# A shorter attention softmax, gate weights in the score buffers, and an instruction order chosen from sixteen

## The chip, the cores and the metric

The kernel runs on one core of a Trainium2 chip. The metric is the device time of one execution in microseconds; before the change it is 1131.54 us, the median of three runs (1131.02 to 1131.56). The engines have names in the profile: PE is TensorE (PEld its weight loads), DVE is VectorE, ACT is ScalarE, POOL is GpSimd, and SP is SyncE, whose queue issues all DMAs of this kernel.

## The reference

One inference step of a decoder with two layers, for a prompt of 512 tokens and eight samples of one token, all in float32. Layer 0 is a gated linear recurrence (HGRN2) with 16 heads of 128; layer 1 is sliding-window attention with 32 query heads of 64, four key and value heads, a window of 128 and a sink per head. Each layer ends with a gate on a per-layer embedding. The attention of the prompt, cut to its core:

```python
def sink_softmax(s, sinks):
    sink = sinks.astype(jnp.float32).reshape(KV_HEADS, Q_PER_KV)[:, :, None, None]
    sink = jnp.broadcast_to(sink, s.shape[:-1] + (1,))
    pr = jax.nn.softmax(jnp.concatenate([s, sink], axis=-1), axis=-1)
    return pr[..., :-1]

    def one_block(args):
        qn, kn, vn, n = args
        mask = in_band & ((cidx >= WINDOW) | (n > 0))
        s = jnp.einsum('bqhgd,bkhd->bhgqk', qn.astype(jnp.float32), kn.astype(jnp.float32)) * ATTN_SCALE
        s = jnp.where(mask, s, -jnp.inf)
        pr = sink_softmax(s, sinks)
        return jnp.einsum('bhgqk,bkhd->bqhgd', pr, vn.astype(jnp.float32))
...
        h = h + rmsnorm(mix, post_norm_g[l])
        h = h + (p[l] @ w_pe[l]) * jax.nn.sigmoid(h @ w_pg[l])
```

## The kernel before

Activations lie transposed: 128 features on the partitions, 520 tokens (512 of the prompt, 8 samples) in a row. A float32 matmul is made of three products of a high and a low half: `wh` and `wl` are the halves of a weight tile of 128 x 512, made by a cast on ACT and a subtraction on DVE (or POOL) from the raw tile `wr`, which a DMA loads. `stream` runs through all projection tiles; `piece` loads a raw tile of 128 x 1024 (tag `wr`, two buffers) and splits half of it. A projection tile is accumulated in `pj`, a pair of PSUM banks, two buffers; all other matmuls use the four banks `ph`.

The attention is computed in eight units of four query heads; each unit has four blocks of 128 queries (`block`, line 1153 on). In a block, PE makes the scores of 128 queries against up to 256 keys (`ph<-xr,g`, keys in `xr`, split queries in `g`), ACT copies one half of the keys and DVE lays the other half over it under a mask, so that 128 scores per query remain in the tile `W` (printed as `b`, in the buffers `b3` or `b2`). Then comes the softmax: a maximum (`an`), three small instructions with the sink, exponentials with an accumulated sum (`ad`), one exponential of the sink (`ae`), an addition, a reciprocal and a multiply. PE transposes `W` (`ph<-ident,b`), ACT and DVE split the result into `g`, and PE multiplies it with the values (`ph<-g,b`). The halves of the result lie on different partitions and are added into `ao`, by way of a copy `m`. Around the blocks PE has the projections of later units and the output projections of earlier ones (`pj<-xs` and `pj<-og`). After units 3 and 7 the attention of the samples runs (`sample_b`, tiles `qs`, `bd`, `bm`).

The gate tiles (`gates`) take pairs of weight tiles; every second pair is marked `spare`, and its halves go to the buffers `b4` of the recurrent layer's state instead of `wh` and `wl`. Its raw tile was still a `wr`.

The order of all this is not written by hand. Every operation is recorded by `enter` with a price, and `issue` (line 200 on) is a list scheduler: engine by engine it takes the ready operation that can start first by its prices and hand-off times, with main work ranked against side work, and puts it into the program. Each engine then works through its own queue in that order; a late operand holds back all that is behind it in the same queue. All instructions carry the line of the helper that records them, 162, so the groups are told apart by tile names.

Of the kernel before, what the change touches and what calls it, by code (L numbers as in the profile page):

```python
# [18 lines left out]
P = 128  # L19
# [12 lines left out]
NEG = -1.0e30  # L32
# [24 lines left out]

WINDOW, LOADS = 1200, 400
# [11 lines left out]
class Slots:  # L70


    def __init__(self, tag, bufs):
        self.free = [0.0] * bufs
        self.keep = next((k for t, k in KEEP.items() if tag == t), max(1, bufs // 2))
        self.order, self.at = [], 0


class Plan:
# [120 lines left out]
    def issue(self):  # L200
        clock = dict.fromkeys(("tensor", "vector", "scalar", "gpsimd", "sync"), 0.0)
# [60 lines left out]
        while todo:  # L262
# [8 lines left out]
            self.tc.keep_in_program_order(op.calls[n]())  # L271
# [46 lines left out]
        self.end = max(clock.values())  # L318
# [39 lines left out]
class Step:  # L358
# [53 lines left out]
    def more_consts(self):  # L412
        nc, cp, i = self.nc, self.cp, self.i
        self.ident = cp.tile([P, P], F32, name="ident")
        nc.sync.dma_start(self.ident, i["ident"])
        self.pairmask = cp.tile([P, 64], F32, name="pairmask")
        nc.sync.dma_start(self.pairmask, i["pairmask"])
        self.ones_r = cp.tile([P, P], F32R, name="ones_r")
        nc.scalar.copy(self.ones_r, self.ones.to_broadcast([P, P]))
        self.lmask = self.plan.tile(self.sp, [P, 6, 64], I32, "lmask", "m", 1)  # L420
        nc.sync.dma_start(self.lmask.rearrange("p a b -> p (a b)"), i["lmask"])
        self.neg = cp.tile([P, 1], F32, name="neg")
        nc.vector.memset(self.neg, NEG)
# [64 lines left out]
    def piece(self, order, n):  # L488
# [76 lines left out]
    def rsqrt_small(self, ps, rows, cols, n, tag):  # L565
        nc = self.nc
        ms = self.small(tag + "m", [P, 8])
        nc.vector.tensor_scalar(ms[:rows, :cols], ps, 1.0 / n, EPS, op0=ALU.mult, op1=ALU.add)
        r = self.small(tag + "r", [P, 8])
# [521 lines left out]
    def unit_proj(self, u, xs, st, done):  # L1091
# [61 lines left out]
    def block(self, u, st, n, osb):  # L1153
# [6 lines left out]
        W = self.small("b3", [P, 4, P], 2) if n % 3 else self.small("b2", [P, 4, P], 3)  # L1160
        for a in range(2):
# [5 lines left out]
            w = W[:, 2 * a : 2 * a + 2]  # L1167
            if n == 0:
# [4 lines left out]
                    self.neg.unsqueeze(1).to_broadcast([P, 2, P]),  # L1173
# [453 lines left out]
```

## Time and profile before

| what | value |
|---|---|
| median of three runs | 1131.54 us |
| profiled execution | 1133.34 us |
| its span, first to last instruction | 1131.5 us |
| mean granted PE clock | 0.995 |
| DMA, mean over the span | 122 GB/s |
| HBM read, written | 119.22 MB, 16.77 MB |

The profiled execution took 1.8 us more than the span that its records cover. The granted clock is the share of full speed that TensorE was allowed; it is 1.00 nearly everywhere. By the 40 slices of the page the recurrent layer fills the time to about 590 us, its norm, gates and the keys and values the time to 690 us, the attention that to 1040 us, and the rest is output projection, norm and gates.

### The profile page before, as it was taken

To read this page: it belongs to the slowest core of one execution; us is meant where nothing else is said; L and a number is where in the kernel's file an instruction comes from. 1 tells how busy PE (TensorE), PEld (TensorE's weight loads), DVE (VectorE), ACT (ScalarE), POOL (GpSimd) and SP (SyncE) were. 2 spreads that over 40 slices of the span, in tenths; PEclk is the share of its full clock that TensorE was granted. 3 is DMA by queue.
4 is the path that set the end of the run, shared out by engine and by line. 5 is a ranking of instruction groups with operands and counts; after the bars stand their busy time and mean duration, and the time that the engine had idled before them with its cause. 6 is when DMAs were issued, how large, how long until landed. Compare 5 with 4: busy or idle time off the path is not lost.

```text
span 1131.5 us, 23984 instructions
## 1 busy us (share of the span) xinstructions
PE 1106.6 (98%) x8999; PEld 1088.3 (96%) x8999; DVE 966.1 (85%) x2218; ACT 749.7 (66%) x1990; POOL 121.8 (11%) x188
## 2 busy tenths in 40 slices
PE   8999999999999999999999999999989999999998
PEld 7999999999999999999999999999989999999997
DVE  6998888758888588888879989999988998998983
ACT  7878777657775477777736657767666764764551
POOL 0121121112211122111100000110100000000000
PEclk9999999999999999999999999999989999999999
DMA  8433524334432343434445442212212222312532
GB/s 292 150 135 115 187 99 170 110 136 152 139 126 97 118 165 134 143 125 138 141 151 204 127 152 91 77 57 86 84 39 75 76 75 75 107 49 73 205 104 86
DMA packets 53821, 137.56 MB, mean 122 GB/s; under 512 B 10948, under 2 KB 18124, under 8 KB 53704
## 3 DMA queue, kind: packets, MB, share of 16 engines
q1 hardware_dynamic: 53704, 136.02, 35.7%
q8 instruction: 71, 1.16, 0.4%
q14 instruction: 46, 0.38, 0.1%
HBM read 119.22 MB, written 16.77 MB: 120 GB/s over the span
## 4 chain that ended last, share of the span: by engine, by line
PE 70%; DVE 20%; ACT 5%; issue 3%; DMA 1%; POOLq 0%; SPq 0%; POOL 0%; DVEq 0%; ACTq 0%
PE pj L162 56%; PE ph L162 14%; DVE g L162 4%; DVE tmp L162 3%; DVE wl L162 3%; DVE b L162 2%; ACT b L162 1%; DVE ao L162 1%; DVE an L162 1%; DVE xr L162 1%; DMA wr<-in_w_pg 1%; DVE x L162 1%; ACT tmp L162 1%; ACT g L162 1%; ACT wh L162 1%
## 5 line engine op out<-in xcount | busy, mean ns | idle before, releaser
L162 PE MATMUL pj<-xs,wh 128*128 128x260 f32 x3328 | 571.2, 285 | 0.8 <-DVE x L162 0.3
L162 PEld LDWEIGHTS pj<-xs,wh 128*128 128x128 f32 x3328 | 468.9, 189 | 4.1 <-ACT xs L162 1.2
L162 PE MATMUL pj<-xs,wl 128*128 128x260 f32 x1664 | 346.6, 285 | 0.0
L162 PEld LDWEIGHTS pj<-xs,wl 128*128 128x128 f32 x1664 | 260.7, 189 | 0.8
L162 ACT CAST wh<-wr 128x512 fp32r<-128x512 f32 x288 | 176.3, 618 | 97.9 <-PE pj L162 87.0
L162 DVE TENSOR_TENSOR wl<-wr,wh 128x512 fp32r<-128x512 f32 x273 | 188.1, 692 | 31.3 <-ACT wh L162 29.9
L162 PE MATMUL pj<-og,wh 128*128 128x260 f32 x1056 | 187.3, 287 | 2.5 <-ACT g L162 1.4
L162 PEld LDWEIGHTS pj<-og,wh 128*128 128x128 f32 x1056 | 152.9, 190 | 4.7 <-DVE x L162 1.8
L162 PE MATMUL pj<-og,wl 128*128 128x260 f32 x512 | 108.0, 286 | 0.0
L162 ACT ACTIVATE tmp<-pj 128x520 f32<-128x520 f32 (+1 forms) x93 | 48.0, 528 | 55.0 <-PE pj L162 54.5
L162 PEld LDWEIGHTS pj<-og,wl 128*128 128x128 f32 x512 | 81.3, 190 | 0.6
L162 ACT ACTIVATE sb<-sb,nv 128x128 f32<-128x128 f32 x128 | 68.4, 564 | 0.2
L162 ACT ACTIVATE sb<-sb,g 128x128 f32<-128x128 f32 x128 | 64.3, 561 | 4.5 <-DVE sb L162 4.2
L162 DVE COPY_PREDICATED xr<-lmask,ph 128x128 f32<-128x128 int32 x192 | 55.2, 323 | 5.3 <-PE ph L162 4.1
L162 PE MATMUL pj<-xs,b 128*128 128x260 f32 x384 | 52.2, 285 | 2.8 <-ACT b L162 2.0
L162 DVE TENSOR_TENSOR x<-x,pj 128x520 f32<-128x520 f32 (+1 forms) x80 | 46.0, 582 | 10.6 <-PE pj L162 9.9
L162 ACT ACTIVATE b<-b,an 128x128 f32<-128x128 f32 x128 | 50.4, 396 | 2.9 <-DVE an L162 2.7
L162 PEld LDWEIGHTS pj<-xs,b 128*128 128x128 f32 x384 | 48.2, 188 | 3.9 <-ACT b L162 2.4
L162 PE MATMUL ph<-g,b 128*128 128x512 f32 x112 | 46.1, 424 | 3.5 <-DVE g L162 2.6
L162 PE MATMUL ph<-b,xr 128*128 128x256 f32 (+1 forms) x288 | 47.5, 281 | 0.0
L162 DVE TENSOR_TENSOR xr<-xr,b 128x256 f32<-128x256 f32 x96 | 41.2, 430 | 4.8 <-PE ph L162 3.0
L162 ACT COPY xr<-ph 32x64 f32<-32x64 f32 (+2 forms) x128 | 39.7, 313 | 8.5 <-PE ph L162 6.1
(208 smaller groups left out, 1861.6 us busy)
## 6 DMA issues: line engine op xcount, KB each, us to landing
wr<-in_w_in_a SPq DMA_DIRECT2D x64, 512.0 KB, 3.6
sb<-sd SPq DMA_DIRECT2D x32, 512.0 KB, 4.7
wr<-in_w_in_b SPq DMA_DIRECT2D x32, 512.0 KB, 3.5
sb<-in_state SPq DMA_DIRECT2D x16, 512.0 KB, 5.0
out_st_s<-sb SPq DMA_DIRECT2D x16, 512.0 KB, 2.9
wr<-in_w_out_a SPq DMA_DIRECT2D x16, 512.0 KB, 3.8
wr<-in_w_pg SPq DMA_DIRECT2D x16, 512.0 KB, 4.3
wr<-in_w_out_b SPq DMA_DIRECT2D x16, 512.0 KB, 3.5
```

Source lines behind the costliest of these rows:

```text
L162: op = Op(len(self.ops), self.level, on, [lambda c=c: c(*a, **k) for c in calls], [self.price(e, name, ins, a, k) for e in on], on[0] == " ...
```

## The change

The softmax is turned around. The query halves are multiplied by minus the scale when they are split, the tile `W` has a 129th column that holds minus the sink, and a minimum over the 129 columns is directly the bias of the exponentials; their accumulated sum then holds the sink's term. The two copies of 64 rows into `m` become one copy of 128 rows, and the additions read PSUM on the other half of the partitions. Masked scores are set to a large positive number.

The raw tiles of `spare` gate weights lie in `b3`, the two buffers of the score tiles, instead of `wr`.

The scheduler's loop is now `arrange`, with each price varied by 2% by a random factor (the first of sixteen orders without). `run` plays each order three times, with durations and hand-offs varied at random and other hand-off times, and `issue` keeps the order with the lowest mean.

```diff
+ONE = {"tensor": -0.3, "vector": 0.115, "scalar": 0.03, "gpsimd": 0.1}
+OTHERS = {"tensor": 0.205, "vector": 0.135, "scalar": 0.165, "gpsimd": 0.17}
+VARY, LATE = 0.03, 0.025
+ORDERS, DIFFER, TRIALS = 16, 0.02, 3
...
     def issue(self):
+        self.uses = self.left
+        orders = [self.arrange(n) for n in range(ORDERS)]
+        times = [np.mean([self.run(order, n) for n in range(TRIALS)]) for order in orders]
+        self.end = min(times)
+        for op, n in orders[times.index(self.end)]:
+            op.engine = op.on[n]
+            self.tc.keep_in_program_order(op.calls[n]())
...
+    def arrange(self, seed):
+        rng = np.random.default_rng(seed)
+        differ = 1 + DIFFER * rng.standard_normal(len(self.ops)) * (seed > 0)
...
+            cost *= differ[op.n]
...
+        nc.vector.tensor_scalar(self.sinkb, self.sinkb, -1.0, None, op0=ALU.mult)
...
-            w.raw = self.plan.tile(self.wp, [P, KC * P], F32, self.name("wr"), "wr", 2)
+            if w.spare:
+                w.raw = self.small("b3", [P, KC * P], 2)
+            else:
+                w.raw = self.plan.tile(self.wp, [P, KC * P], F32, self.name("wr"), "wr", 2)
...
-        ms = self.small(tag + "m", [P, 8])
+        bufs = 1 if tag == "nn" else 2
+        ms = self.small(tag + "m", [P, 8], bufs)
...
-                    nc.scalar.copy(s[me, :SEQ], q[me, :SEQ])
-                    nc.vector.tensor_tensor(
-                        s[other, :SEQ], q[me, :SEQ], s[me, :SEQ].bitcast(F32), op=ALU.subtract
+                    nc.scalar.activation(s[me, :SEQ], q[me, :SEQ], AF.Copy, scale=-SCALE)
+                    nc.vector.scalar_tensor_tensor(
+                        s[other, :SEQ], q[me, :SEQ], -SCALE, s[me, :SEQ].bitcast(F32), op0=ALU.mult, op1=ALU.subtract
...
-        W = self.small("b3", [P, 4, P], 2) if n % 3 else self.small("b2", [P, 4, P], 3)
+        W = self.small("b3", [P, 4, P + 1], 2) if n % 3 else self.small("b2", [P, 4, P + 1], 3)
+        nc.scalar.copy(W[:, :, P], self.sinkb[:, 4 * u : 4 * u + 4])
...
-        nc.vector.tensor_reduce(nm, W, AX.X, ALU.max)
-        sk = self.sinkb[:, 4 * u : 4 * u + 4]
-        nc.vector.scalar_tensor_tensor(nm, nm, SCALE, sk, op0=ALU.mult, op1=ALU.max)
-        es = self.small("ae", [P, 4])
-        nc.vector.tensor_tensor(es, sk, nm, op=ALU.subtract)
-        nc.vector.tensor_scalar(nm, nm, -1.0, None, op0=ALU.mult)
+        nc.vector.tensor_reduce(nm, W, AX.X, ALU.min)
         den = self.small("ad", [P, 4])
         for j in range(4):
             nc.scalar.activation(
-                W[:, j], W[:, j], AF.Exp, bias=nm[:, j : j + 1], scale=SCALE, accum_out=den[:, j : j + 1]
+                W[:, j], W[:, j], AF.Exp, bias=nm[:, j : j + 1], scale=-1.0, accum_out=den[:, j : j + 1]
             )
-        nc.scalar.activation(es, es, AF.Exp)
-        nc.vector.tensor_tensor(den, den, es, op=ALU.add)
         nc.vector.reciprocal(den, den)
+        W = W[:, :, :P]
...
+        nc.scalar.copy(both, po)
         for a in range(2):
...
-            t = both[:, a * 256 : (a + 1) * 256]
-            nc.scalar.copy(t[me], po[other, a * 256 : (a + 1) * 256])
-            nc.vector.tensor_tensor(
-                osb[me, :, n * P : (n + 1) * P],
-                po[me, a * 256 : (a + 1) * 256].rearrange("p (c t) -> p c t", c=2),
-                t[me].rearrange("p (c t) -> p c t", c=2),
-                op=ALU.add,
-            )
+            of = lambda x, rows: x[rows, a * 256 : (a + 1) * 256].rearrange("p (c t) -> p c t", c=2)
+            nc.vector.tensor_tensor(osb[me, :, n * P : (n + 1) * P], of(po, other), of(both, me), op=ALU.add)
```

What this does to the order, at three places. First PE, where the last block of unit 3 and the first sample attention meet. Before, `ph_2059` are the transposes of that block, `ph_2064` its products with the values, `ph_2147` scores of unit 4, and `ph_2101` the samples' products:

```order
L162 MATMUL ph_2147<-xr_1774,g_2088 128x256
L162 MATMUL ph_2147<-xr_1778,g_2088 128x256
L162 MATMUL ph_2147<-xr_1774,g_2089 128x256
L162 MATMUL ph_2147<-xr_1778,g_2089 128x256
L162 MATMUL ph_2059<-ident,b_1957_2053 128x128 x4
L162 MATMUL ph_2064<-g_2060,b_1652_1748 128x512
L162 MATMUL ph_2101<-tmp_2100,b_1995_2091 128x16 x8
L162 MATMUL ph_2064<-g_2061,b_1652_1748 128x512
L162 MATMUL ph_2064<-g_2062,b_1653_1749 128x512
```

After the change the same block's transposes are `ph_2047`; its products with the values (`ph_2052`) begin after three more rows:

```order
L169 MATMUL ph_2047<-ident,b_1946_2042 128x128 x4
L169 MATMUL ph_2111<-xr_1774,g_2076 128x128
L169 MATMUL ph_2111<-xr_1778,g_2076 128x128
L169 MATMUL ph_2111<-xr_1774,g_2077 128x128
L169 MATMUL ph_2111<-xr_1778,g_2077 128x128
L169 MATMUL pj_2100<-xs_1702,wh_2072 128x260
L169 MATMUL pj_2100<-xs_1702,wl_2073 128x260 x2
L169 MATMUL ph_2082<-ident,tmp_2081 128x128
L169 MATMUL pj_2100<-xs_1703,wh_2072 128x260
L169 MATMUL ph_2121<-xr_1774,g_2076 128x256
L169 MATMUL ph_2121<-xr_1778,g_2076 128x256
L169 MATMUL ph_2121<-xr_1774,g_2077 128x256
```

The transposes had their own products directly behind them, and now have scores of the next unit and projections (`pj_2100`) there.

Second DVE at the same place: the queue in front of the multiply by the reciprocal, whose result the transposes read. Before (`an`, `ae`, `ad` of three blocks, 2058 being the one in question):

```order
L162 SCALAR_TENSOR_TENSOR an_2124<-an_2124,sinkb 128x4
L162 TENSOR_TENSOR ao_2015<-ph_2051,m_2052 64x2x128
L162 TENSOR_TENSOR ae_2125<-sinkb,an_2124 128x4
L162 TENSOR_SCALAR an_2124<-an_2124 128x4
L162 TENSOR_TENSOR ad_2058<-ad_2058,ae_2057 128x4
L162 TENSOR_REDUCE an_2135<-b_2036_2132 128x4
L162 RECIPROCAL ad_2058<-ad_2058 128x4
L162 SCALAR_TENSOR_TENSOR an_2135<-an_2135,sinkb 128x4
L162 TENSOR_TENSOR b_1957_2053<-b_1957_2053,ad_2058 128x512
```

After the change, the rows up to the multiply of the same block:

```order
L169 RECIPROCAL ad_2046<-ad_2046 128x4
L169 COPY_PREDICATED b_2013_2109<-pmask,far 128x2x128
L169 TENSOR_TENSOR tmp_2074<-tmp_2074,tmp_2075 128x520
L169 TENSOR_TENSOR g_2039<-g_2037,tmask 128x512
L169 TENSOR_TENSOR wl_2096<-wr_2094,wh_2095 128x512
L169 SCALAR_TENSOR_TENSOR g_2076<-tmp_2074,g_2076 64x512
L169 SCALAR_TENSOR_TENSOR g_2077<-tmp_2074,g_2077 64x512
L169 TENSOR_TENSOR ao_2007<-ph_2040,m_2041 64x2x128 x2
L169 TENSOR_TENSOR b_1946_2042<-b_1946_2042,ad_2046 128x4x128
```

The small instructions are gone from in front of it; wide ones of the projections stand there instead.

Third the queue of SP at the gates of layer 1. Before, from the fifth output write on:

```order
L162 DMA out_yT<-og_2697 128x260
L162 DMA out_yT<-og_2698 128x260
L162 DMA wr_2816<-in_w_pg 128x1024
L162 DMA wr_2818<-in_w_pg 128x1024
L162 DMA out_yT<-og_2699 128x260
L162 DMA out_yT<-og_2700 128x260
```

After the change, the last four loads of gate weights and the first output writes:

```order
L169 DMA wr_2771<-in_w_pg 128x1024
L169 DMA wr_2774<-in_w_pg 128x1024
L169 DMA b_2688_2784<-in_w_pg 128x1024
L169 DMA b_2690_2786<-in_w_pg 128x1024
L169 DMA out_yT<-og_2665 128x260
L169 DMA out_yT<-og_2666 128x260
```

The last two loads stood behind six output writes, and all loads now stand ahead of the first one.

More of the change, by code (lines that the diff above doesn't have):

```diff
@@ L200, in issue, with run, ready @@
     def issue(self):
+        self.uses = self.left
[5 more added lines that the diff above has]
+            self.tc.keep_in_program_order(op.calls[n]())
+    def run(self, order, seed):
+        rng = np.random.default_rng(seed)
+        vary = 1 + VARY * rng.standard_normal(len(order))
+        late = np.abs(LATE * rng.standard_normal(len(order)))
+        queues = {e: [] for e in ("tensor", "vector", "scalar", "gpsimd", "sync")}
+        place = {op: i for i, (op, n) in enumerate(order)}
+        on = {op: op.on[n] for op, n in order}
+        cost = {op: op.cost[n] for op, n in order}
+        last, users = {}, {}
+        for op, n in order:
+            queues[on[op]].append(op)
+            for t in op.tiles:
+                last[t] = op
+                users.setdefault(t, []).append(op)
+        homes = {t: tag for tag, s in self.slots.items() for t in s.order}
+        free = {tag: [None] * s.bufs for tag, s in self.slots.items()}
+        over = {}
+        for t, op in last.items():
+            over.setdefault(op, []).append(t)
+        before = {}
+        for op, n in order:
+            old = [free[tag].pop(0) for tag, t in op.news]
+            before[op] = [d for t in old if t for d in users[t]]
+            for t in over.get(op, ()):
+                free[homes[t]].append(t)
+        end, clock, at = {}, dict.fromkeys(queues, 0.0), dict.fromkeys(queues, 0)
+        pipe, lanes, port, slow = 0.0, [0.0] * 16, 0.0, 0.0
+        def ready(op, e):
+            t = clock[e]
+            for deps, tile in ((op.deps, False), (before[op], True)):
+                for d in deps:
+                    if d not in end:
+                        return None
+                    if tile and on[d] == e and not op.dma:
+                        continue
+                    t = max(t, end[d] + (0.1 if d.dma else (ONE if on[d] == e else OTHERS)[on[d]]))
+            return t + late[place[op]] * (t > clock[e])
+        heads = {}
+        for _ in order:
+            for e, q in queues.items():
+                if heads.get(e) is None and at[e] < len(q):
+                    heads[e] = ready(q[at[e]], e)
+            t, r, e = min(
+                (max(r, port) if cost[queues[e][at[e]]][1] else r, r, e) for e, r in heads.items() if r is not None
+            )
+            op = queues[e][at[e]]
+            long = cost[op][0] * vary[place[op]]
+            if op.dma:
+                t = max(t, lanes[0])
+                clock[e] = t + 0.45
+                pipe = max(pipe, t + 1.4) + long
+                end[op] = pipe + 1.6
+                lanes = sorted(lanes[1:] + [end[op]])
+            else:
+                if e == "tensor":
+                    if t - clock[e] > IDLE:
+                        slow = t + SLOW
+                    if t < slow:
+                        long *= 2
+                end[op] = clock[e] = t + long
+                if cost[op][1]:
+                    port = end[op]
+            at[e] += 1
+            heads[e] = None
+        return max(end.values())
@@ L317, in issue @@
                         stale.add(x)
-        self.end = max(clock.values())
+        return order
 class Planned:
```

24 lines of the change are left out of this document (16 added, 8 removed).

## The prediction

> **What bounds the kernel now.** I read the page's busy line first, then the busy times by stretch, then what TensorE (PE) waited for in each stretch, and last the timeline at the longest wait.
>
> ```profile
> span 1131.5 us, 23984 instructions
> PE 1106.6 (98%) x8999; PEld 1088.3 (96%) x8999; DVE 966.1 (85%) x2218; ACT 749.7 (66%) x1990; POOL 121.8 (11%) x188
> ```
>
> PE is the bound: it is busy 98% of the span, and the change leaves every matmul in place. So nothing can be won but PE's gaps and its slow clock. By stretch (stretch, length, busy time of PE, PEld, DVE, ACT and POOL, granted PE clock, DMA):
>
> ```profile
> 20.00:590.00 570.00, 568.79 (x4757) 568.07 (x4756) 470.51 (x1054) 404.10 (x1014) 94.84 (x163) 1.00 0.40 136
> 590.00:690.00 100.00, 97.51 (x798) 95.64 (x798) 90.58 (x232) 60.01 (x150) 4.46 (x4) 1.00 0.48 161
> 690.00:820.00 130.00, 126.81 (x1009) 122.64 (x1008) 125.90 (x282) 89.89 (x263) 13.28 (x10) 1.00 0.24 79
> 820.00:840.00 20.00, 16.44 (x93) 14.97 (x92) 15.59 (x48) 13.34 (x55) 0.00 (x0) 0.74 0.09 27
> 840.00:1040.00 200.00, 198.43 (x1585) 193.43 (x1584) 182.60 (x420) 127.09 (x393) 5.19 (x4) 1.00 0.23 75
> 1040.00:1131.50 91.50, 83.99 (x672) 81.15 (x670) 67.45 (x159) 38.80 (x88) 3.70 (x2) 0.99 0.37 128
> ```
>
> From 20 to 590 us, the recurrent layer, PE misses 1.2 us of 570; nothing is to be had there. The attention fills 690 to 1040 us. There VectorE (DVE) is nearly a second bound, 125.9 us of 130 in the first stretch, and 20 us in the middle ran at a granted clock of 0.74. PE's gaps from 690 to 1040 are 3.2 + 3.6 + 1.6 = 8.3 us (length less busy). The two largest sums of what it waited for there (total, times, longest):
>
> ```profile
> PE ph L162 <- DVE ae L162: 3.4, 2, 2.9
> PE ph L162 <- DVE g L162: 2.6, 4, 0.9
> ```
>
> Both come from DVE. Four of the 8.3 us belong to one place, where unit 3 ends and the first sample attention runs:
>
> ```profile
> 816.88 0.63 PE L162 MATMUL ph<-ident,b 128*128 128x128 f32 x4 [0.55 <-DVE b L162]
> ...
> 822.42 1.13 PE L162 MATMUL ph<-xr,g 128*128 128x256 f32 x8
> 826.43 0.88 PE L162 MATMUL ph<-ident,b 128*128 128x128 f32 x4 [2.88 <-DVE ae L162]
> 827.99 0.79 PE L162 MATMUL ph<-g,b 128*128 128x512 f32 x1 [0.67 <-ACT g L162]
> ```
>
> PE's queue is in order, and what stands next waits 2.88 us for the softmax of the last block (ident,b are its transposes), then 0.67 us for the cast of their result. Those waits are 0.55 + 2.88 + 0.67 = 4.1 us. The low clock: 0.26 of 20 us is 5.2 us of lost clock, that is about 10.4 us at half speed; 0.67 us of it was a wait anyway, so 9.7 us did the work of 4.9 us, and 4.9 us were lost. This one place costs 9.0 us, more than all other gaps of the attention (8.3 - 4.1 = 4.2 us).
>
> **Part 1: the shorter softmax.** Every one of the 32 blocks loses four small DVE instructions and one ACT exponential; one ACT copy of the sink is added, and two 64-row copies become one of 128 rows.
>
> ```profile
> L162 DVE SCALAR_TENSOR_TENSOR an<-an,sinkb 128x4 f32<-128x4 f32 x32 | 6.0, 189 | 0.2
> L162 DVE TENSOR_TENSOR ae<-sinkb,an 128x4 f32<-128x4 f32 x32 | 5.9, 187 | 0.2
> L162 DVE TENSOR_SCALAR an<-an 128x4 f32<-128x4 f32 x32 | 5.3, 164 | 0.5
> L162 DVE TENSOR_TENSOR ad<-ad,ae 128x4 f32<-128x4 f32 x32 | 4.9, 156 | 2.5 <-ACT b L162 2.1
> ...
> L162 ACT ACTIVATE ae<-ae 128x4 f32<-128x4 f32 x32 | 6.2, 198 | 8.1 <-DVE ae L162 7.9
> L162 ACT COPY m<-ph 64x256 f32<-64x256 f32 x64 | 23.5, 367 | 13.2 <-PE ph L162 10.6 <-DVE ao L162 1.7
> L162 ACT COPY tmp<-ph 128x512 f32<-128x512 f32 x2 | 1.2, 586 | 1.1 <-PE ph L162 1.0
> L162 ACT COPY zb<-g 128x8 f32<-128x8 f32 x16 | 3.1, 195 | 4.2 <-DVE g L162 3.9
> ```
>
> DVE gives up 6.0 + 5.9 + 5.3 + 4.9 = 22.1 us. ACT gives up 6.2 us and 23.5 - 32 x 0.586 = 4.7 us, and takes on 32 x 0.195 = 6.2 us for the sink's copies: 4.7 us less. The negated scale in the query's split makes a cast an ACTIVATE and a subtraction a SCALAR_TENSOR_TENSOR; neither form at 64 x 512 is in the trace. The nearest rows bound both:
>
> ```profile
> L162 DVE TENSOR_TENSOR g<-tmp,g 64x512 fp32r<-64x512 f32 x32 | 23.0, 718 | 1.8 <-ACT g L162 0.6
> L162 DVE TENSOR_TENSOR g<-ph,g 128x512 fp32r<-128x512 f32 x32 | 21.7, 685 | 1.4 <-ACT g L162 1.2
> L162 DVE SCALAR_TENSOR_TENSOR ao<-ao,g 128x512 f32<-128x512 f32 x16 | 10.5, 686 | 0.1
> L162 ACT CAST xs<-xr 128x260 fp32r<-128x260 f32 x18 | 7.1, 407 | 3.4 <-DVE xr L162 3.3
> L162 ACT ACTIVATE g<-xr,vec 128x260 fp32r<-128x260 f32 x12 | 6.1, 509 | 5.0 <-DVE xr L162 5.0
> L162 ACT ACTIVATE tmp<-x 128x260 f32<-128x260 f32 x14 | 5.8, 422 | 3.3 <-DVE x L162 3.3
> ```
>
> The DVE form at 128 x 512 costs the same as the subtraction (686 against 685 ns). The 64-row subtraction is 33 ns slower than the full one (718 against 685), and I let the new form lie 33 ns to either side of it, 1.1 us in 32; I take 0. The ACT form costs 15 ns (422 - 407) to 102 ns (509 - 407, with a factor per row) more: 0.5 to 3.3 us in 32; I take the lower, since the new factor is a constant as in the 422 ns row. ACT is busy 127 us of 200 in the attention, and that slack covers either end. The 129-column rows of the score tile add one element in 128 to the exponentials and the minimum: under 0.3 us; an odd row pitch is not in the trace, and I let it cost a block between nothing and twice those 33 ns, 2 us in 32; I take the lower end, to which the unchanged element count is nearest. All of this stands beside PE's work; if DVE had no slack it would appear in the sum.
>
> Here is the same stretch of DVE at the long wait:
>
> ```profile
> 823.43 0.41 DVE L162 TENSOR_TENSOR ao<-ph,m 64x256 f32<-64x256 f32 x1
> 823.77 0.14 DVE L162 SCALAR_TENSOR_TENSOR an<-an,sinkb 128x4 f32<-128x4 f32 x1
> 823.95 0.43 DVE L162 TENSOR_TENSOR ao<-ph,m 64x256 f32<-64x256 f32 x1
> 824.41 0.16 DVE L162 TENSOR_TENSOR ae<-sinkb,an 128x4 f32<-128x4 f32 x1
> ```
>
> The first addition is on rows 0 to 63, and the next instruction starts 0.07 us before it ends; the second is on rows 64 to 127, and neither it nor the instruction after it overlaps its neighbour. Two overlaps in a block are lost so. After the change both additions read PSUM on the other half of the rows than they write, so I count three: 32 x 0.07 = 2.2 us more, and DVE saves about 20 us net (22.1 - 2.2) of the 324 us that it is busy from 690 to 1040.
>
> This is the rule of the Trainium skill, "VectorE: DVE Perf Modes", section "Two Vector instructions with no wait between them": a DVE instruction whose operands start in another quarter of the partitions than those just before it starts only when all earlier ones have ended. The four rows agree with it. If the 2.2 us fell on PE's path the sum below would be 10.5 instead of 12.7 us; while DVE has 350 - 304 = 46 us to spare there they don't.
>
> What the saving is worth is read from the waits. At 826 us the transposes wait for a multiply that stands, in the order printed above, behind six small instructions, five of which go away; and the changed order has other matmuls around the same block's transposes. I take this place's 9.0 us as gained. Of the other 4.2 us, mostly products that wait for DVE's halves (DVE g), the same queue in front is shorter, but the order is new and will have tight places of its own: I take a third, **1.4 us**.
>
> **Part 2: raw gate weights in other places.** Eight of the sixteen gate loads go to the two score buffers, which stand empty at that time, so four raw tiles can be in flight.
>
> ```profile
> 651.50 0.62 ACT L162 CAST b<-wr 128x512 fp32r<-128x512 f32 x1 [1.38 <-DMA wr<-in_w_pg]
> 652.17 0.39 PE L162 MATMUL pj<-xs,b 128*128 128x260 f32 x1 [0.85 <-ACT b L162]
> ...
> 1089.51 12.76 SPq L162 DMA_DIRECT2D out_yT<-og  x6
> 1102.39 0.94 SPq L162 DMA_DIRECT2D wr<-in_w_pg  x2
> ...
> 1109.28 0.39 PE L162 MATMUL pj<-xs,b 128*128 128x260 f32 x1 [1.15 <-ACT b L162]
> 1110.00 0.39 PE L162 MATMUL pj<-xs,b 128*128 128x260 f32 x1 [0.34 <-DVE b L162]
> ...
> 1110.00 17.41 PE pj L162 x143
> ```
>
> The last two gate loads stood in SP's queue behind six output writes that took until 1102.27 to be issued; the cast came late and PE waited 1.15 + 0.34 us. In layer 0 it waited 0.85 us for the same reason. The changed order issues these loads ahead of all output writes. The gain is 0.85 + 1.15 + 0.34 = 2.3 us; next late is nothing, since from 1110.00 on PE runs through its last 143 matmuls in one piece (the last row, of the chain). Queued behind a load that waits for its score buffer are only the output writes, and they are not needed before the end.
>
> **Part 3: the order.** Sixteen orders with costs varied by 2% are built, and the best in a trial with varied durations is kept. PE's content is the same. Where PE had no waits there is nothing to gain, and it can lose: I take 0, between the 1.2 us of 20 to 590 us gained and as much lost.
>
> **Sum.** 9.0 + 1.4 + 2.3 = 12.7 us. The profiled execution took 1133.34 us, 1.8 us more than its span of 1131.5 and than the median of 1131.54 us of the runs; 1133.34 - 12.7 = 1120.6 there, and **1118.8 us** against the median.
>
> A rule against this: the Trainium skill, "TensorE: Matmul & The Clock Gate", section "Why this matters for your kernels", asks only for no PE gap over about 3 us. By it a gap of 2.88 us would not have lowered the clock. The trace does not agree: the 20 us at 0.74 hold that gap. By the rule the place would be worth its 4.1 us of waits alone, the sum 7.8 us and the time 1123.7 us; I go by the row.
>
> **Rivals.**
> - A long gap again. PE's queue is fixed, and the plan trims the work in front of each block's transposes when the chain gets shorter. If one gap like that of 826 us opens anywhere, it costs 2.88 + 0.67 + 4.9 = 8.5 us: 1127.3 us. For it: 32 blocks, and a place with 2.88 us was planned before too. Against: at the old place other matmuls now stand between. 17%.
> - It doesn't do what it says: the waits are of the plan, not of DVE, and come back as large; only the 2.3 us of the loads are gained: 1129.3 to 1131.5 us. For it: the gaps from 690 to 1040 us are 2% of that time, and an order is made without seeing them. 10%.
> - All waits go: the other 2.8 us of the attention, 1.2 us of 20 to 590, 2.5 - 0.85 = 1.6 us of 590 to 690, and at the last norm the row below, 0.9 us. 1118.8 - 6.5 = 1112.3 us. For it: DVE falls from 97% to about 91% in 690 to 820. Against: the norm is not changed. 15%.
>
> ```profile
> PE ph L162 <- POOL rsr L162: 0.9, 1, 0.9
> ```
>
> - Slower, one mechanism: the shorter chain is planned to its edge, and the ACT copies added in front of the exponentials make it late at each block. The price is 32 times the lateness; from 0.4 us a block on it outweighs the 12.7 us, at 0.6 us it gives 1118.8 + 19.2 = 1138 us. Against: 29 of the 32 transposes did not wait before, with longer chains. 8%.
>
> **Chances.** The forecast holds 50% by itself, 65% with the third rival. The range goes from 1112 (all waits gone) to 1129 us (a long gap again, 1127.3, with the 1.2 us of part 3 on top), 82% in all. A measurement of this kernel can tell about 0.2%, 2.3 us, from no change. Faster by more than that, below 1129.3: 50 + 15 + 17 = 82%; same 10%; slower 8%.
>
> **What would show it.** Right: no stretch of the attention with a clock under 1.00; PE's gaps in it near 2.8 us in total; DVE busy there about 304 us instead of 324; the last gate loads issued before the first output write, and no PE wait for ACT b after 1100 us. Part 1 is wrong if DVE falls so and PE's waits stay; part 3 if waits over 0.5 us appear between 20 and 590 us. The whole is wrong if a second half-clock stretch is seen.

## The result, and the profile after

The changed kernel takes **1121.31 us** (median of 4 runs, 1120.94 to 1121.76), beside 1131.55 us for the kernel before (median of 4 runs, 1131.02 to 1131.84). The ratio is 0.991, with a 95% interval of 0.9893 to 0.9927. The forecast was 1118.8 us, and the time lies in its range. The profiled execution took 1120.95 us. Beside the profiled 1133.34 us of before that is 12.4 us less, where the sum had 12.7; beside the medians it is 10.2 us.

The page of the changed kernel, its span and its busy times:

```profile
span 1119.2 us, 23830 instructions
PE 1100.9 (98%) x8999; PEld 1086.5 (97%) x8999; DVE 948.6 (85%) x2092; ACT 741.9 (66%) x1958; POOL 121.3 (11%) x187
```

The matmuls are the same 8999, and the DVE has 17.5 us less to do (966.1 before). The same stretches as in the prediction, with the same columns (stretch, length, busy time of PE, PEld, DVE, ACT and POOL, granted PE clock, DMA share, GB/s):

```profile
20.00:590.00 570.00, 568.59 (x4748) 567.41 (x4747) 468.83 (x1055) 404.60 (x1013) 93.00 (x161) 1.00 0.41 136
590.00:690.00 100.00, 95.48 (x773) 94.02 (x772) 88.59 (x222) 58.44 (x147) 5.85 (x4) 0.98 0.46 161
690.00:820.00 130.00, 128.56 (x1025) 125.04 (x1024) 126.59 (x255) 91.76 (x271) 12.29 (x10) 1.00 0.25 81
820.00:840.00 20.00, 20.00 (x159) 19.33 (x159) 18.76 (x51) 17.22 (x66) 0.00 (x0) 1.00 0.14 38
840.00:1040.00 200.00, 199.21 (x1608) 195.58 (x1607) 176.64 (x346) 120.09 (x360) 6.87 (x5) 1.00 0.27 89
1040.00:1119.20 79.20, 73.53 (x600) 72.02 (x598) 55.81 (x139) 33.25 (x76) 3.01 (x2) 1.00 0.31 109
```

PE's count in brackets tells where the time went: the stretches are cut by the clock and not by the program, so a kernel that gets more matmuls done in a stretch has won there. One matmul takes about 0.119 us (568.59 / 4748). The differences to before:

| stretch | matmuls before | after | us won (-: lost) |
|---|---|---|---|
| 20 to 590 | 4757 | 4748 | -1.1 |
| 590 to 690 | 798 | 773 | -3.0 |
| 690 to 1040 | 1009 + 93 + 1585 = 2687 | 2792 | +12.5 |
| 1040 to the end | 672 in 91.5 us | 600 in 79.2 us | +3.7 |

The last row is 91.5 - 79.2 us less the 72 matmuls at 0.119 us that already lie behind. The counts take all matmuls as equally long, so they are an estimate. The four sum to 12.1 of the 12.3 us between the spans. The attention gave more than forecast, and the first layer's norm and gates, at 590 to 690 us, took 3.0 us back.

From 690 to 1040 us PE's gaps fell from 8.3 to 1.44 + 0.00 + 0.79 = 2.2 us, and the clock is full. What PE still waited for there (total, times, longest) is this:

```profile
PE ph L169 <- DVE g L169: 1.6, 3, 0.6
PE ph L169 <- DVE b L169: 0.4, 1, 0.4
```

What was lost is in the timeline at the first layer's norm, rows of DVE, POOL and PE. POOL takes the power that makes the reciprocal root (rsr), and PE waits for it:

```profile
612.87 1.29 DVE L169 TENSOR_TENSOR b<-b,b 128x512 fp32r<-128x512 f32 x2
614.07 0.15 DVE L169 TENSOR_SCALAR rsm<-ph 128x3 f32<-128x3 f32 x1
614.14 0.48 DVE L169 SCALAR_TENSOR_TENSOR tmp<-x,vec,R 128x260 f32<-128x260 f32 x1
614.30 3.19 POOL L169 TENSOR_TENSOR rsr<-rsm,mhalf 128x3 f32<-128x3 f32 x1 [7.27 <-DVE rsm L169]
614.54 1.30 DVE L169 TENSOR_TENSOR g<-g,g 128x520 fp32r<-128x520 f32 x2
615.76 0.68 DVE L169 TENSOR_TENSOR wl<-wr,wh 128x512 fp32r<-128x512 f32 x1
616.36 0.42 DVE L169 TENSOR_TENSOR xr<-xr,tmp 128x260 f32<-128x260 f32 x1
616.70 0.88 DVE L169 SCALAR_TENSOR_TENSOR tmp<-x,vec,R 128x260 f32<-128x260 f32 x2
617.50 0.76 DVE L169 TENSOR_TENSOR xr<-xr,tmp 128x260 f32<-128x260 f32 x2
617.54 0.56 PE L169 MATMUL ph<-ident,rsr 128*128 128x128 f32 x3 [2.29 <-POOL rsr L169]
```

The same place in the kernel before:

```profile
612.60 0.15 DVE L162 TENSOR_SCALAR rsm<-ph 128x3 f32<-128x3 f32 x1
612.67 1.52 DVE L162 TENSOR_TENSOR g<-g,g 128x520 fp32r<-128x520 f32 x2
612.83 1.24 POOL L162 TENSOR_TENSOR rsr<-rsm,mhalf 128x3 f32<-128x3 f32 x1 [5.93 <-DVE rsm L162]
614.11 0.68 DVE L162 TENSOR_TENSOR wl<-wr,wh 128x512 fp32r<-128x512 f32 x1
```

The power of three columns took 1.24 us before and 3.19 us after, and after it PE waited 2.29 us. Two splits of gate weights out of the score buffers (b<-b,b, 1.29 us) now stand on DVE directly ahead of the mean that the power needs (rsm), and DVE then works without a pause until the power has ended. It does that in the kernel before too, but there the two subtractions `g<-g,g` stand directly behind the mean, and they take 1.52 us instead of 1.30. From 617.9 us the granted clock is halved for 3.41 us.

At the end the loads did what was forecast. SP's queue there, with the start and length of the issuing:

```profile
1066.94 2.46 SPq L169 DMA_DIRECT2D wr<-in_w_pg  x2
1069.78 0.80 SPq L169 DMA_DIRECT2D b<-in_w_pg  x2
1079.88 36.87 SPq L169 DMA_DIRECT2D out_yT<-og  x16
```

All gate loads are issued before the first output write, and PE waits for no ACT b (halves of gate weights) there any more.

### The profile page after: what moved, and what is told of

It reads as the page before. It is cut to its first block, busy times and chain, and to the rows that moved or that the text cites. A ratio compares the mean times of both kernels' runs of the same rounds, so it can differ in the third digit from the quotient of the medians.

```text
span 1119.2 us, 23830 instructions
## 1 busy us (share of the span) xinstructions
PE 1100.9 (98%) x8999; PEld 1086.5 (97%) x8999; DVE 948.6 (85%) x2092; ACT 741.9 (66%) x1958; POOL 121.3 (11%) x187
## 4 chain that ended last, share of the span: by engine, by line
PE 82%; DVE 11%; ACT 3%; issue 2%; DMA 0%; POOL 0%; POOLq 0%; SPq 0%; DVEq 0%; ACTq 0%
PE pj L169 65%; PE ph L169 17%; DVE tmp L169 2%; DVE g L169 2%; DVE wl L169 2%; DVE xr L169 1%; DVE b L169 1%; DVE x L169 1%; DVE ao L169 1%; ACT b L169 1%; DVE os L169 1%; DVE acc L169 1%; ACT tmp L169 1%; ACT g L169 0%; ACT og L169 0%
## 5 line engine op out<-in xcount | busy, mean ns | idle before, releaser
L169 DVE TENSOR_TENSOR wl<-wr,wh 128x512 fp32r<-128x512 f32 x275 | 190.4, 696 | 43.3 <-ACT wh L169 41.9
L169 ACT ACTIVATE b<-b,an 128x129 f32<-128x129 f32 x128 | 50.7, 399 | 2.4 <-DVE an L169 1.6
L169 DVE TENSOR_TENSOR g<-g,b 128x256 f32<-128x256 f32 x96 | 42.6, 443 | 4.8 <-ACT tmp L169 2.2
```

The source lines that it names most:

```text
L169: op = Op(len(self.ops), self.level, on, [lambda c=c: c(*a, **k) for c in calls], [self.price(e, name, ins, a, k) for e in on], on[0] == " ...
```

## The experiments

Each kernel was timed in five rounds beside the kernel before. The ratio is to that kernel, whose medians were 1132.44, 1131.98 and 1131.81 us in the three sets (the first four, the next four and the last four rows).

| kernel | median us | ratio, 95% interval |
|---|---|---|
| soft_only | 1118.18 | 0.9873 (0.986 to 0.9886) |
| load_only | 1131.06 | 0.9994 (0.9983 to 1.0005) |
| order_only | 1124.11 | 0.9926 (0.9912 to 0.994) |
| first_order | 1123.81 | 0.9922 (0.9909 to 0.9935) |
| after_pow_apart | 1118.55 | 0.9877 (0.9861 to 0.9893) |
| after_load_back | 1138.89 | 1.0059 (1.0047 to 1.0072) |
| before_lean | 1127.09 | 0.9952 (0.9939 to 0.9965) |
| before_filled | 1134.61 | 1.0021 (1.0011 to 1.003) |
| before_filled2 | 1129.16 | 0.9972 (0.996 to 0.9983) |
| soft_late | 1116.44 | 0.9863 (0.985 to 0.9877) |
| late_order | 1116.54 | 0.9863 (0.9849 to 0.9876) |
| soft_late_apart | 1118.89 | 0.988 (0.9865 to 0.9895) |

### The three parts, each by itself

**soft_only** is the kernel before with the softmax lines of the diff alone (the scheduler and the loads as before).

```diff
+        W = self.small("b3", [P, 4, P + 1], 2) if n % 3 else self.small("b2", [P, 4, P + 1], 3)
+        nc.scalar.copy(W[:, :, P], self.sinkb[:, 4 * u : 4 * u + 4])
...
-        nc.vector.tensor_reduce(nm, W, AX.X, ALU.max)
...
+        nc.vector.tensor_reduce(nm, W, AX.X, ALU.min)
```

> The kernel before with the shorter softmax alone (one order, raw gate weights as before). Theory A, DVE's queue in the attention is what PE waited for: most of the gain is here, 1131.5 - 8 to 10 = 1121.5 to 1123.5 us, and no half-clock stretch in the attention. Rival B, the choice among sixteen orders is what pays: within 2 us of 1131.5. Rival C, any new order happens to miss the one bad place: about 1123 us, but then the other two single parts lose that place as well.

**load_only** is the kernel before with the loads alone.

```diff
-            w.raw = self.plan.tile(self.wp, [P, KC * P], F32, self.name("wr"), "wr", 2)
+            if w.spare:
+                w.raw = self.small("b3", [P, KC * P], 2)
+            else:
+                w.raw = self.plan.tile(self.wp, [P, KC * P], F32, self.name("wr"), "wr", 2)
```

> The kernel before with the raw tiles of every second gate pair in the score buffers, nothing else. Theory A: 1.5 to 2.3 us faster, 1129.2 to 1130 us, the wait for ACT b at 1109 us gone and the half-clock stretch at 826 us still there. Rival B: the same as A for this part. Rival C: the half-clock stretch is gone too, about 1121 us.

**order_only** is the kernel before with the choice among sixteen orders alone.

```diff
+ORDERS, DIFFER, TRIALS = 16, 0.02, 3
...
+        orders = [self.arrange(n) for n in range(ORDERS)]
```

> The kernel before with the choice among sixteen orders alone. Theory A: the DVE load is unchanged, so waits of the attention come back in other places; 1127 to 1132 us. Rival B: 1121 to 1124 us. Rival C: about 1123 us, with no half-clock stretch.

**first_order** is the changed kernel with one order.

```diff
-ORDERS, DIFFER, TRIALS = 16, 0.02, 3
+ORDERS, DIFFER, TRIALS = 1, 0.02, 3
```

> The changed kernel with the first, unvaried order in place of the choice among sixteen. Theory A: 1120 to 1123 us, the choice is worth 1 us at most. Rival B: 1128 us or more. Rival C says nothing of it.

The softmax alone is faster than the whole change, and 3.3 us below what theory A gave for it. Two stretches of soft_only:

```profile
590.00:690.00 100.00, 97.42 (x796) 95.53 (x796) 90.38 (x231) 60.37 (x154) 4.46 (x4) 1.00 0.48 160
820.00:840.00 20.00, 19.73 (x161) 19.22 (x160) 18.31 (x49) 17.79 (x65) 0.00 (x0) 1.00 0.17 54
```

Its first layer is that of before (796 matmuls against 798), and the place at 820 to 840 us is at full clock. The loads alone gain nothing clear of the noise, and in load_only the norm shows the stall of the changed kernel:

```profile
613.43 3.19 POOL L162 TENSOR_TENSOR rsr<-rsm,mhalf 128x3 f32<-128x3 f32 x1 [6.45 <-DVE rsm L162]
616.68 0.71 PE L162 MATMUL ph<-ident,rsr 128*128 128x128 f32 x3 [2.30 <-POOL rsr L162]
```

In the first layer, first_order has it too (3.18 us); soft_only and order_only, without these loads, do not. The order alone keeps a good part of the slow clock at the old place (0.17 of 20 us, which is 6.8 us at half speed):

```profile
820.00:840.00 20.00, 18.47 (x118) 17.33 (x117) 17.50 (x56) 14.45 (x57) 1.36 (x1) 0.83 0.10 30
```

The loads alone have full clock there, with the old softmax:

```profile
820.00:840.00 20.00, 17.68 (x126) 15.62 (x126) 18.87 (x56) 15.46 (x57) 0.00 (x0) 1.00 0.21 67
```

PE's longest wait around that place is 2.88 us in the kernel before, 1.58 us in load_only, 1.17 us in order_only and 0.3 us in soft_only. So rival C holds in part: any other order that was run loses the wait of 2.88 us, and in load_only's profiled execution the half clock is gone too. That is not the whole gain of the attention. By the counts from 690 to 1040 us, order_only wins 6.0 us (2737 matmuls against 2687) and load_only 6.4 us (2741), but soft_only 12.5 us (2792), as much as the whole change.

The parts do not add up: 14.3 us for the softmax, 1.4 for the loads (no difference by their interval) and 8.3 for the order, each by itself against the 1132.44 us of its set, and 10.2 together. All three change the same place. Order_only lies at the upper edge of rival B's range, 3 us below theory A's. Within the change, the choice is worth 1123.81 - 1121.31 = 2.5 us by the medians, where 1 us at most was expected, but the two ratios' intervals overlap.

### What makes the power slow

**after_pow_apart** keeps the order of the changed kernel. In the second half of each layer's norm ahead of the gates the mean, the power and a copy of one column are issued together, so that DVE stands still while POOL works.

```diff
+    def apart(self, r, mean, root):
+        self.tc.keep_in_program_order(mean())
+        self.tc.keep_in_program_order(root())
+        return self.plan.nc.vector.tensor_scalar(r[:, 7:8], r[:, 2:3], 1.0, None, op0=ALU.mult)
```

> The changed kernel in its own order, but VectorE waits out the power of the second half of each norm (one column copied behind it), so that nothing of VectorE runs beside it. Theory (the power on POOL takes 3.19 us at 614.3 because VectorE is busy without a gap beside it, where it takes 0.85 to 1.24 us elsewhere): both powers take 0.8 to 1.3 us, TensorE's wait of 2.29 us for it falls below 0.8 us, the half clock at 617.9 is gone, and the time falls by 2 to 4 us, to 1117.3 to 1119.3. Rival (the power is long for a reason of its own, or what is late there is the queue ahead of it): it stays near 3.2 us, VectorE stands still as long, TensorE waits more than 2.3 us, and the time is 1122 to 1125.

Its rows at the norm, and the stretch around it:

```profile
615.08 0.85 POOL L169 TENSOR_TENSOR rsr<-rsm,mhalf 128x3 f32<-128x3 f32 x1 [7.28 <-DVE rsm L169]
615.96 0.15 DVE L683 TENSOR_SCALAR rsr<-rsr 128x1 f32<-128x1 f32 x1 [0.96 <-POOL rsr L169]
```

```profile
590.00:690.00 100.00, 97.08 (x796) 95.25 (x795) 90.69 (x232) 60.23 (x154) 3.45 (x4) 1.00 0.48 166
```

The theory holds. The power takes 0.85 us, the clock stays full in this stretch, PE no longer waits for the power, 23 of the 25 lost matmuls are back (796 against 773), and the time falls by 2.8 us although DVE stands still 0.96 us. So it is DVE's work beside it that makes this power slow. Such work is not enough by itself: beside DVE without a pause the same power took 1.24 us in the kernel before, and the first half's power took 0.85 us in the changed kernel (at 606.18 us). The Trainium skill, "SBUF — State Buffer", section "Who interferes with whom", names a pair of ports that VectorE and GpSimd share as an exclusive lock. The rows agree that one holds up the other (the power 3.19 us in the changed kernel, the two subtractions 1.52 instead of 1.30 us in the kernel before), and don't show at which moment POOL gets its turn.

### What VectorE's work is worth in the attention

**after_load_back** keeps the order of the changed kernel and adds four small additions on DVE behind each block's minimum.

```diff
+            call = lambda: v.tensor_tensor(self.junk, self.junk, self.mhalf[:, :4], op=ALU.add)
...
-        nc.vector.tensor_reduce(nm, W, AX.X, ALU.min)
+        op = nc.vector.tensor_reduce(nm, W, AX.X, ALU.min)
+        op.calls = [lambda c=op.calls[0]: self.more(c)]
```

> The changed kernel in its own order, with four additions of 128x4 on VectorE behind each block's minimum: VectorE gets about the work back that the change took off it, the path from scores to weights does not get the links back. Theory (the attention gained because VectorE had less to do): TensorE's gaps between 690 and 1040 rise from 2.2 us to 5 or more, and the time to 1125 to 1130. Rival (it gained because the path is shorter, and VectorE has room): gaps below 3.5 us and 1121 to 1123.

The added group (times, busy us, mean ns) and the three stretches of the attention:

```profile
L681 DVE TENSOR_TENSOR junk<-junk,mhalf 128x4 f32<-128x4 f32 x128 | 22.5, 176 | 3.3
```

```profile
690.00:820.00 130.00, 121.82 (x958) 117.00 (x957) 126.76 (x285) 87.84 (x256) 11.15 (x9) 1.00 0.24 78
820.00:840.00 20.00, 19.30 (x156) 18.57 (x156) 19.08 (x53) 14.99 (x54) 0.20 (x1) 1.00 0.08 27
840.00:1040.00 200.00, 193.59 (x1534) 187.41 (x1533) 178.79 (x411) 121.16 (x372) 7.39 (x5) 1.00 0.23 75
```

The gaps rise from 2.2 to 8.18 + 0.70 + 6.41 = 15.3 us, and the time by 1138.89 - 1121.31 = 17.6 us, for 22.5 us of work. The theory holds, and by more than it had (1125 to 1130 us): DVE's busy share of 92% in the changed kernel's attention is no room for work at this place. A small part may be the path and not the load, since ACT's exponentials wait for the additions in two places, 1.0 us in all. Another caveat is that this order was not made with the additions in view; the kernel before carried about as much work in an order made for it, with 8.3 us of gaps.

**before_lean** keeps the order of the kernel before and does not issue four of the links: they are planned as before and then left out. The negated maximum is made in one step, and the sink's share is missing from the sums.

```diff
+        skip = [nc.vector.scalar_tensor_tensor(nm, nm, SCALE, sk, op0=ALU.mult, op1=ALU.max)]
...
+        skip.append(nc.vector.tensor_tensor(es, sk, nm, op=ALU.subtract))
+        neg = nc.vector.tensor_scalar(nm, nm, -1.0, None, op0=ALU.mult)
+        neg.calls = [lambda: self.plan.nc.vector.tensor_scalar(nm, nm, -SCALE, None, op0=ALU.mult)]
...
+        skip.append(nc.scalar.activation(es, es, AF.Exp))
+        skip.append(nc.vector.tensor_tensor(den, den, es, op=ALU.add))
+        for op in skip:
+            op.calls = [lambda: None]
```

> The kernel before in its own order, without the three VectorE and one ScalarE instructions per block that bring the sink into the softmax (the sink's share is left out of the sums). Theory (the links themselves made the waits): the waits of 690 to 1040, 8.3 us and the half clock, fall to 3 us or less without half clock, and the time to 1119 to 1123. Rival (the fixed order of the queues makes the waits, and the gain of the softmax change is what the planner does with it): at least half of the waits stay, the half clock at 826 stays, and the time is 1127 to 1131.

```profile
823.12 0.63 PE L162 MATMUL ph<-ident,b 128*128 128x128 f32 x4 [2.84 <-DVE an L1187]
```

```profile
820.00:840.00 20.00, 16.33 (x101) 14.98 (x100) 15.66 (x43) 13.87 (x53) 0.00 (x0) 0.83 0.08 27
```

The rival held, at the lower edge of its range. 4.9 us are gained, but the long wait stays at 2.84 us (2.88 before), with 6.83 of its 10.24 us of half clock. Of the 8.3 us of gaps from 690 to 1040 us 6.0 stay (1.48 + 3.67 + 0.84). Without the small instructions ahead of the multiply those transposes come hardly earlier, because something else is as late. The chain of work that ended in them shows what (start, length; the multiply is the last row):

```profile
819.79 0.36 ACT m L162
...
820.18 1.27 ACT b L162 x6
...
821.47 0.69 DVE an L162
...
822.28 0.69 DVE b L162
```

Exponentials on ACT stand behind a copy `m`, and a wide minimum of another block stands between them and the multiply on DVE. From the copy to the multiply it takes 2.49 us, where the kernel before takes 2.57 (823.03 to 825.60). Outside 820 to 840 us the gaps halve without the links (4.8 to 2.3 us); the long wait goes only with another order.

### What the wait at 826 us costs

**before_filled** and **before_filled2** keep the order of the kernel before and add twelve matmuls of 128x512 ahead of the transposes of one block, into the bank that these then overwrite.

```diff
+        for _ in range(12):
+            self.tc.keep_in_program_order(self.plan.nc.tensor.matmul(pt, K[:, :P], K, start=True, stop=True))
```

> The kernel before in its own order, with twelve more matmuls of 128x512 (some 2.8 us) in the place of the wait of 2.88 us at 825: they write the bank that the transposes then write over. Theory (the wait is what halves the clock, and the half clock costs 4.9 us): the clock stays full and the time falls by 4 to 5 us, to 1126.5 to 1127.5. Rival (the clock halves for the load of that stretch or the gap moves behind the added matmuls): half clock still seen, and 1131 to 1134.5.

This one missed its place: the code counts units from zero, and the matmuls ran at 858 us, in the block one unit on, where PE did not wait. It gives only their price, 1134.61 - 1131.98 = 2.6 us. The second has them where the wait is.

> The kernel before in its own order, with the twelve added matmuls of 128x512 (2.6 us, as the first try in another block measured them at full clock) now directly ahead of the transposes that wait 2.88 us at 826. Theory (the wait makes the half clock, and it costs 4.9 us): the wait shrinks to 0.3 us or less, the clock stays at 1.00, and the time falls by 4 to 5 us, to 1126.5 to 1128. Rival (the half clock comes of what runs there, not of the wait): it is still seen, and the time is 1131 to 1134.

```profile
821.38 2.90 PE L1240 MATMUL ph<-xr 128*128 128x512 f32 x12
824.34 0.66 PE L162 MATMUL ph<-ident,b 128*128 128x128 f32 x4
825.67 0.50 PE L162 MATMUL ph<-g,b 128*128 128x512 f32 x1 [0.68 <-ACT g L162]
826.46 2.15 PE L162 MATMUL ph<-tmp,b 128*128 128x16 f32 x16 [0.29 <-DVE g L162]
```

The wait is gone, since the added work covers it, and of the 10.24 us at half clock 6.83 are gone too; 3.41 us remain, beginning at 828.1 us, after waits of only 0.68 and 0.29 us and during the samples' matmuls of 16 columns. The time falls by 2.65 us, and lies between the two ranges. So both theories hold in part: two thirds of the half clock (6.83 us, or 3.4 of the predicted 4.9 us) came of the long wait. Whether the rest comes of the two short waits or of the samples' matmuls was not told apart.

### The loads in the last layer alone

**soft_late** is soft_only with the loads in the last layer only; **late_order** is the changed kernel with that limit.

```diff
+        for w in ws:
+            w.late = w.spare and layer == 1
...
-            if w.spare:
+            if w.late:
```

> The kernel before with the shorter softmax, and raw gate weights in the places of the scores in the last layer alone; one order. Theory (the loads help where the prediction had 1.15 + 0.34 us, at the end, and harm in the first layer, where they press the splits into the norm): no half clock at 617, waits near 610 to 620 as in the kernel before, and the time is 1 to 2 us below that of the softmax alone: 1116 to 1117.5. Rival (they are worth nothing at the end either, since PE waits elsewhere): 1118 to 1120.

> The changed kernel, choice of sixteen orders included, with raw gate weights in the places of the scores in the last layer alone. Theory (the loads of the first layer cost the changed kernel the wait for the power, the half clock and the waits beside it, about 3 us): no half clock at 617, and the time is 1117.3 to 1118.8. Rival (the order that is chosen puts splits beside the power all the same): half clock and wait stay, 1120 to 1122.

The choice among sixteen takes the first order for late_order, and the instructions of the two kernels are the same, engine by engine. They are two measurements of one program, 1116.44 and 1116.54 us, 4.8 us below the changed kernel and the best that was run. Both theories hold, late_order below its range, and the choice among orders adds nothing here. The first layer is whole again, here in late_order:

```profile
590.00:690.00 100.00, 98.37 (x808) 96.85 (x807) 91.64 (x234) 60.30 (x155) 4.45 (x4) 1.00 0.48 163
```

Against soft_only the loads at the end win 1.7 us by the medians of two sets, with overlapping intervals, so that gain is not shown.

**soft_late_apart** is soft_late with the edit of after_pow_apart.

> As the kernel with the softmax and the loads of the last layer alone, and VectorE waits out the power of the second half of each norm. Theory (TensorE waits 0.9 us for the power of the last norm, which takes 2.85 us beside VectorE): it takes 0.8 to 1.3 us there, that wait goes, and the time is 0.7 to 1.5 us below that kernel: 1115 to 1116.5. Rival (standing still costs VectorE as much as the power gains): the same time within 0.5 us, or more.

The rival held. Both powers take 0.85 us, and the time is 2.4 us more. In the first layer the power took only 1.24 us without the edit, and DVE's standing still makes the embedding's products late:

```profile
614.54 1.38 PE L162 MATMUL pj<-g,wh 128*128 128x260 f32 x6 [1.18 <-DVE g L162]
```

From 614.9 us the clock was then halved for 3.41 us. So keeping DVE still paid where its work had kept POOL waiting long (3.19 us), and cost time where the power had been short.

## Why the prediction came out as it did

- **PE is the bound, and only gaps and the slow clock can be won: right in the main.** PE's idle time fell by 6.6 us (24.9 to 18.3 in the span), and 6.83 us less at half clock are worth up to 3.4 us. The other 2.3 of the 12.3 us lie in PE's busy time and were not told apart.
- **The sum of 12.7 us came out at 12.1 by counts, in part by luck:** the attention gave 2.1 us more than its two terms, and the last layer more than its term, while the first layer lost 3.0 us that had no term.
- **The place at 826 us, 9.0 us: gone as forecast, but only one of the two reasons given holds.** The prediction laid the wait on the small instructions ahead of the multiply; before_lean takes four of the links away and keeps the wait, since the exponentials on ACT are as late. Its other reason, the other order around the transposes, holds: order_only and load_only, with the old softmax, shorten the wait to 1.17 and 1.58 us. No run has the shorter softmax in the old order. Of the 4.9 us for the half clock, before_filled2 shows 3.4 us to belong to the wait.
- **The attention's other gaps, 1.4 us: 2.0 us** (4.2 to 2.2). By counts the attention gave 12.5 us, where the two terms had 10.4.
- **"While DVE has 350 - 304 = 46 us to spare": wrong as an argument.** after_load_back spends 22.5 us of that room and PE loses 17.6 us. By that run the idle time of DVE does not lie where the work is. That the three lost overlaps fall beside PE's work was therefore not shown.
- **DVE at 304 us from 690 to 1040: 322.0 us** (126.59 + 18.76 + 176.64). The window holds 105 matmuls more of the program, which the sign left out of account; for the same reason DVE stays at 97% from 690 to 820 us (126.59 of 130), where 91% was forecast. The whole span tells it better: 17.5 us less, where 20 were forecast.
- **The forms without a row in the trace** came out inside their bounds. The groups of the changed kernel (times, busy us, mean ns):

```profile
L169 DVE SCALAR_TENSOR_TENSOR g<-tmp,g 64x512 fp32r<-64x512 f32 x32 | 21.9, 686 | 1.1 <-ACT g L169 0.2
L169 DVE TENSOR_REDUCE an<-b 128x4 f32<-128x516 f32 x32 | 21.8, 681 | 0.3
L169 ACT ACTIVATE g<-tmp 64x512 fp32r<-64x512 f32 x32 | 20.2, 630 | 10.9 <-DVE tmp L169 10.4
```

  The split's subtraction became 32 ns shorter (718 to 686), the odd row pitch costs nothing (679 to 681), and the cast's new form costs 11 ns, where 15 were taken.
- **The gate loads, 2.3 us: this is the step that failed.** "Next late is nothing" was argued for the end alone. There the waits of 1.15 and 0.34 us went; the whole stretch won 3.7 us, and what made the rest was not told apart. In the first layer the 0.85 us went too, but with the earlier raw weights DVE has two splits directly ahead of the mean and other work directly behind it, and the power took 3.19 us: 25 matmuls or 3.0 us lost. load_only shows the same with the loads alone; after_pow_apart and late_order each give it back by their own way.
- **The order, 0 us:** 1.1 us lost by counts from 20 to 590, inside the bound (0.2 us of it are gaps of PE); PE's longest wait there is 0.5 us, at the sign's edge and not over it.
- **The rival of a long gap again** had the mechanism, in another place and smaller: 2.29 us of wait and 1.7 us of clock. The prediction wrote that a second half-clock stretch would make the whole wrong. It was seen, and the whole stood, because the stretch was 3.41 us and not 10.
- **The rule of the Trainium skill, "TensorE: Matmul & The Clock Gate", section "Why this matters for your kernels"**, was set aside for the row of 2.88 us. That was right: half clock followed again on a wait of 2.29 us (after) and on one of 1.18 us (soft_late_apart).
- **1.8 us taken off for the median: this is where 2.2 us of the miss of 2.5 us lie.** The profiled execution of before lay 1.8 us above its median, that of after 0.4 us below (1120.95 beside 1121.31). So the 12.4 us between the two are 10.2 us between the medians.

## What to carry to other kernels

When transfers come earlier, ask what their consumers will now stand in front of: here it moved ahead of and beside a small operation of another engine that PE waits for. Try each part of a change by itself, and each part at each place where it acts; here one part was worth more than the whole, and another harmed in one layer, while its gain in the other is within the noise. When a scheduler makes the order, any change makes another order: compare with one that leaves the mechanism alone, before a vanished wait is credited to the mechanism. Busy shares under 100% are no proof of room on an engine whose queue is in order.

## What the runs showed of the hardware

- A power of 128x3 on POOL took 0.85 us with DVE at rest (all four held ones in after_pow_apart and soft_late_apart). Beside DVE it took 0.85 us (after, 606.18), 1.24 us (before, 612.83) or up to 3.19 us (after, 614.30), each time with DVE busy without a pause. What decides between these was not shown.
- The granted clock halves in pieces of 3.41 us and multiples of it. At the place in the attention they are 10.24 us in the kernel before, 6.83 in order_only and before_lean, and none in the changed kernel, which has 3.41 us at the norm; after_pow_apart, before_lean and late_order have one more of 3.41 us in the first 20 us of their profiled executions. The length of a wait alone does not decide: 1.18 us was followed by 3.41 us at half clock in soft_late_apart, and the samples' place in load_only, with a wait of 1.58 us ending at 824.8, stayed at full clock in its profiled execution. The Trainium skill, "TensorE: Matmul & The Clock Gate", section "What's actually happening", has a window of 3413 ns that runs freely and does not begin with the kernel. The lengths agree with it, and so does the time from the first full clock to the first half clock, 822.61 us in before and 610.99 us in after, 241 and 179 such windows.
- One program's times can differ with the granted clock: the twelve of load_only lie at 1129.5 to 1130.0 us with a mean granted clock of 0.996 to 0.998 (six), and at 1132.1 to 1133.8 us with 0.991 to 0.994 (six). That the window's phase makes the two was not tried.
